# Issuing the four column-position matmuls of the modulation product as one group that waits for its four transfers

## The chip, the cores and the metric

The kernel runs on one core of a Trainium2 chip. The metric is the device time of one execution in microseconds (us): the median of three runs before the change is 3344.96 us (3344.82 to 3346.26). The engines are TensorE (PE in the profile, with PEld for its weight loads), VectorE (DVE), ScalarE (ACT), GpSimd (POOL) and SyncE (SP), which here only issues transfers.

## What is computed

Two transformer blocks of two layers each run over 512 tokens of 1024 features. Nearly all the time goes to products with large weights. The change touches one small product of the second block: per layer, a column vector and its context counterpart are passed through silu and multiplied with a weight of 1024 x 6144, and the result gives shifts, scales and gates.

```python
def modulate(h, shift, scale):
    return h * (1.0 + scale) + shift

silu_c = jax.nn.silu(c)              # c: 1024 features
silu_cc = jax.nn.silu(c_ctx)
for layer in range(DEPTH):           # 2 layers
    mod_x = silu_c @ ada_w[layer] + ada_b[layer]      # ada_w[layer]: 1024 x 6144
    mod_c = silu_cc @ ada_w[layer] + ada_b[layer]
    sh1, sc1, g1, sh2, sc2, g2 = [m[:, None, :] for m in jnp.split(mod_x, 6, axis=-1)]
    csh1, csc1, cg1, csh2, csc2, cg2 = jnp.split(mod_c, 6, axis=-1)
    hx = modulate(rmsnorm(x, norm1_g[layer]), sh1, sc1)
    ...
    x = x + g1 * (mx @ w_out[layer])
```

Neither `c` nor `c_ctx` depends on the first block, so this product can be made long before it is needed.

## The kernel before

`net` emits the parts of the program one after the other: loading, the first mixer (`mixer0`), the modulation and the context beside it, memory attention (`mem_attention`), the MLP, the second mixer, and the second block. A scheduler in the framework then reorders what was emitted: each engine gets one fixed order of instructions, in which an instruction stands where the scheduler's own timing says that its operands are there. On the chip each engine works through its order, and a wait at the head holds up what is queued behind it.

`linear` and `linear_tm` make the large products. `wload` (L227) brings a chunk of weights (tile `raw`, a transfer that SP issues on L237), ACT copies it to `whi` (L241) and DVE forms the rest `wlo` (L242). `mat3` then makes three matmuls in a fast 32-bit format (`hi` and `lo` are halves of the activations). All of them are recorded on L159.

`modulation` (L1001) is emitted through `beside`: with `side` set, its tiles come from a storage of their own, 20 buffers of 128x512 in the tag `b2`, some of which hold other things for long (the memory's keys and values), and its sums go to one PSUM bank, `bank`. It makes six sums one after the other (two layers l, three parts b). Each sum has eight steps k over the 1024 inputs, and each step has four matmuls, one for each 512 columns of the weight. A matmul has the 128x32 tile `sil[:, k]` as weights (two of its 32 columns hold the two vectors) and the 128x512 tile `ada` as moving data, in full 32-bit format; it uses 32 columns of the array. The four of a step stand on the four column positions 0, 32, 64 and 96 (`tile_position=(0, 32 * g)`). So there are 2 x 3 x 8 x 4 = 192 such matmuls (L1023) and 192 transfers of 256 KB (L1022), which SP issues in the same queue as the `raw` transfers. The profile records each of these matmuls as two, so its counts are twice these: "x2" is one matmul, "x8" four. When a sum is done, ACT copies it (`modr`, L1028), PE transposes it (L171), and DVE adds the bias (L1038).

Of the kernel before, what the change touches and what calls it, by code (L numbers as in the profile page):

```python
# [19 lines left out]
KT = 8  # L20
# [35 lines left out]
class Half:  # L56
    """a half of the tokens of a list of pairs of tiles, which may grow"""
# [16 lines left out]
class Stream:  # L74
    """A part of the program that is emitted in steps: it yields how long its next step's operands take,
    or a condition that has to hold before its next step."""
# [5 lines left out]
class Net:  # L82
# [21 lines left out]
    # ---- storage  # L104
# [22 lines left out]
    def b2(self, dt=F32, nm="t", w=T):  # L127
        """a tile of the storage of the streams beside the main one"""
        side, self.side = self.side, True
        t = self.t2(dt, nm, w)  # L130
        self.side = side
        return t
# [22 lines left out]
    # ---- tensor engine  # L155
# [5 lines left out]
    def mat3(self, out, a, b, start, stop, shared=False):  # L161
        """The product of two exact sums of halves, all but that of the low halves.
        shared: other sums are under way in the bank, and only its first matmul has start set."""
        k = {"skip_group_check": True} if shared else {}
        self.mat(out, a[0], b[0], start, False, **k)
        self.mat(out, a[0], b[1], False, False, **k)
        self.mat(out, a[1], b[0], False, stop, **k)
# [5 lines left out]
    # ---- banks that a stream holds over several of its steps  # L173
# [12 lines left out]
    def beside(self, gen):  # L186
        """emits a stream that has storage of its own, which so runs whenever the others wait"""
        self.side = True
        for _ in gen:
            pass  # L190
        self.side = False

    # ---- order of emission: the first stream whose operands should be there goes on
# [32 lines left out]
    # ---- weights: a chunk of up to 1024 columns as an exact sum of two float32r tiles  # L226
# [19 lines left out]
    def linear(self, w, k0, kn, c0, cn, segs, evac, xo=0, apart=0, gate={}):  # L246
        """Feature-major: output tile m has 128 features on partitions and the tokens of a segment.
        segs: (list of (hi, lo), width), narrow segments first; evac(m, tile), or evac(m, tile, segment).
        xo: the inputs begin with this one of a segment's list.
        apart: for so many of the steps of columns (the first if positive, else the last), one segment comes  # L250
        after the other; gate: instructions that are queued before the n-th group of products, by n."""
        nk = kn // 128
        step = min(cn, 256)
        kc = min(nk, (T if self.side else WCH) // step)
        nm = step // 128
        blocks, ns = range(0, nk, kc), cn // step
        order = [(i, kb, s) for i in range(ns) for kb in blocks for s in range(len(segs))]
        n = abs(apart) * len(blocks) * len(segs)
        a = 0 if apart > 0 else len(order) - n
        order[a:a + n] = sorted(order[a:a + n], key=lambda t: t[2])  # L260
        pss, halves, groups = {}, {}, 0
        for at, (i, kb, s) in enumerate(order):
            xs, wd = segs[s]
            if len(xs) < xo + kb + kc:
                yield lambda: len(xs) >= xo + kb + kc
            shared = wd * nm <= T
            if kb == 0:
                yield from self.take("mm", 1 if shared else nm)
                if shared:
                    p = self.mm((128, nm, wd))  # L270
                    pss[i, s] = [p[:, m] for m in range(nm)]
                else:
                    pss[i, s] = [self.mm((128, wd)) for _ in range(nm)]
            if (i, kb) not in halves:
                r0, c = k0 + kb * 128, c0 + i * step
                halves[i, kb] = self.wload(w[r0:r0 + kc * 128, c:c + step], kc, step)
            hi, lo = halves[i, kb]
            ps = pss[i, s]
            for m in range(nm):
                with self.tc.issue_after(gate[groups]) if groups in gate else nullcontext():  # L280
                    for k in range(kb, kb + kc):
                        a = (hi[:, k - kb, sl(m)], lo[:, k - kb, sl(m)])
                        self.mat3(ps[m], a, xs[xo + k], k == 0 and not (shared and m), k == nk - 1, shared)
                groups += 1
            if kb + kc == nk:
                for m in range(nm):
                    evac(i * nm + m, ps[m], *([s] if len(segs) > 1 else []))
                self.give("mm", 1 if shared else nm)
            if s == len(segs) - 1 or order[at + 1][0:2] != (i, kb):
                yield 0.0  # L290

    def halves(self, w, segs, add, swap=False):
        """A product with all of the square w in two parts, that of the first four inputs (the rows of w from
        the middle on, if swap) and that of the others; add(m, tile, last)."""
# [3 lines left out]
    def linear_tm(self, w, k0, kn, c0, cn, xs, ntok, evac, cut=1):  # L298
        """Token-major: 128 tokens on partitions; evac(i, tile of tokens i and features c0...)."""
# [22 lines left out]
    # ---- pieces of norms  # L322
    def rsqrt(self, m):
        """m ** -1/2 of a small tile, refined by a Newton step"""
# [14 lines left out]
    def rows(self, r, n, copy=True):  # L339
        """a value of every token (tokens on partitions, column i for tile i), on all partitions"""  # L340
# [12 lines left out]
    def sq_add(self, st, x, w=T, half=None):  # L353
        """adds x * x to the running tile in the list st, or to a half of it"""
# [9 lines left out]
    def token_rows(self, st, w=T, copy=True):  # L364
        """1/sqrt(mean + eps) of every token, the same on all partitions"""
        return self.rows(self.token_cols(st, w)[1], w // 128, copy)

    def token_cols(self, st, w=T):
        """mean square + eps and its reciprocal root, tokens on partitions: column i for tile i"""
# [7 lines left out]
    def pair(self, w, nm=("hi", "lo")):  # L377
        """room for the two halves of w columns"""
# [5 lines left out]
    def hpair(self):  # L384
        """room for the halves of a normalized tile of the residual stream"""
# [5 lines left out]
    def split(self, x, g=None, w=T, rows=128, pair=None):  # L391
        """x (times a column g) as an exact sum of two float32r tiles"""
# [10 lines left out]
    # ---- residual stream  # L403
# [16 lines left out]
    def add_x(self, m, p, restore=False, norm=None):  # L420
        """x tile m += p; restore: from the order of columns of the grid to that of rows;
        norm: gains (name, layer) of the norm that follows"""
# [16 lines left out]
    # ---- keys and values of the memory  # L439
# [114 lines left out]
    # ---- squared-ReLU MLP of the first block  # L554
# [32 lines left out]
    # ---- first mixer: pooling and latent attention  # L587
    def mixer0(self):
# [81 lines left out]
        def rotate(x, q, rot):  # L670
            """x: tokens of tiles 2 q and 2 q + 1, heads, 32 features, times their gains"""
# [149 lines left out]
    def pipe(self, streams, width):  # L821
        """a stream made of others, of which width are under way at a time"""
# [30 lines left out]
    # ---- second mixer: neighbourhood attention, tokens in the order of columns  # L853
    def mixer1(self):
# [18 lines left out]
        def project(g, o):  # L873
            """queries, keys and values of heads 4 g to 4 g + 3"""
# [126 lines left out]
    # ---- second block: modulation, columns of shift, scale and gate for both streams  # L1001
    def modulation(self):
# [11 lines left out]
        for l in range(2):  # L1014
            mod = self.cst(f"mod{l}", [128, 48, 2])
            for b in range(3):
                yield from self.take("mm")
                p = self.mm()
                for k in range(KT):
                    for g in range(4):  # L1020
                        w = self.t2(nm="ada")
                        nc.sync.dma_start(w, A["ada_w_2"][l, sl(k), b * 2048 + g * 512:b * 2048 + (g + 1) * 512])  # L1022
                        nc.tensor.matmul(p[32 * g:32 * g + 32], lhsT=sil[:, k], rhs=w,  # L1023
                                         start=(k == 0), stop=(k == KT - 1), tile_position=(0, 32 * g))
# [23 lines left out]
    def mod_h(self, l, j, st, xs, sums, w):  # L1048
        """normalized and modulated stream st for sublayer j, as exact halves"""
# [16 lines left out]
    def mod_c(self, l, j):  # L1066
        """mod_h of the context without DVE"""
# [21 lines left out]
    def mod_half(self, l, j, half, h):  # L1089
        """mod_h for a half of the tokens of x"""  # L1090
# [15 lines left out]
    def context(self):  # L1106
        """the context and what its first mixer needs"""
# [22 lines left out]
    # ---- decays of the retention heads and other constants of the scans  # L1130
    def decay_consts(self):
# [19 lines left out]
        # decay of a key to the end (or start) of its chunk  # L1151
# [13 lines left out]
    def decay_tables(self, l):  # L1165
        """decays of a query from its chunk's start (or end), and between query and key in a chunk"""
# [15 lines left out]
    # ---- hybrid mixer: decaying retention and gated linear attention  # L1182
    def hybrid(self, l, h, w, st_in, st_out, outputs, rot, y):
        """the streams of the mixer; its outputs, tiles of 128 features, go to the list y"""
# [35 lines left out]
        def narrow(nm):  # L1220
            """tiles of w columns"""
# [47 lines left out]
        def finish(key, hd, p, ln):  # L1269
            """normalization of a head's output (tokens on partitions), its gate, and back to features"""  # L1270
# [319 lines left out]
    def final(self, half):  # L1590
        """the last norm of a half of the tokens; GpSimd multiplies what DVE has no time for"""
# [18 lines left out]
def shape_tables():  # L1610
    """constants that depend on the shapes alone"""
# [109 lines left out]
```

## Time and profile before

| | |
|---|---|
| median of 3 runs | 3344.96 us |
| span of the profiled execution | 3351.3 us |
| PE busy | 3268.7 us, 98% |
| DVE busy / ACT busy | 1784.2 us, 53% / 1204.7 us, 36% |
| DMA | 323.99 MB, mean 97 GB/s |
| first and last start of a modulation matmul | 191.5 and 483.9 us |

The profiled execution's own time is not listed beside its span; the span is 6.3 us above the median of the runs. A row of the timeline gives the start, the length, the engine, the line, the tiles (written<-read) and a count of instructions that follow each other. The end of a matmul is modelled, so lengths of neighbours overlap; what a matmul takes from the engine is the distance from its start to the start of the next one.

### The profile page before, as it was taken

The page shows a single profiled execution, that of the slowest core. Times are in us where ns is not written, and L with a number is a line of the kernel's source. Part 1 is how long each engine was busy: PE and PEld are TensorE (multiplying, and loading weights), DVE is VectorE, ACT ScalarE, POOL GpSimd, SP SyncE. Part 2 cuts the span into 40 slices and gives each one's busy share as a digit, 9 for nine tenths or more (in the row PEclk, how much of TensorE's full clock was granted, in tenths as well). Part 3 has the DMA queues.
Part 4 walks back from the last instruction along what each step waited for, and adds up shares of the span by engine and source line. Part 5 has one row for each costly group of instructions (what it writes and reads, how often), then busy time and mean ns, then how long its engine had stood idle before and what let it go on. Part 6 is the DMA issues. An engine that isn't in the chain of part 4 may idle for free.

```text
span 3351.3 us, 45020 instructions
## 1 busy us (share of the span) xinstructions
PE 3268.7 (98%) x17942; PEld 2675.4 (80%) x17942; DVE 1784.2 (53%) x3208; ACT 1204.7 (36%) x2157; POOL 207.9 (6%) x257
## 2 busy tenths in 40 slices
PE   8999999999999999999999999999999989899998
PEld 8745448888988778888888987888888879788887
DVE  6853126444555646444776587333334755774444
ACT  5732224222444443222553354221322533433323
POOL 0100000000011100000011212000000011200000
PEclk9999999999999999999999999999999999899999
DMA  5356542332322123333442321222221433123332
GB/s 154 119 165 213 190 149 89 98 97 95 117 60 85 63 67 94 96 99 95 135 121 76 89 83 59 68 63 63 63 63 59 122 89 88 51 64 98 97 94 76
DMA packets 301858, 323.99 MB, mean 97 GB/s; under 512 B 18832, under 2 KB 270608, under 8 KB 301648
## 3 DMA queue, kind: packets, MB, share of 16 engines
q1 hardware_dynamic: 296656, 315.22, 30.9%
q10 hardware_dynamic: 4992, 5.90, 0.6%
q8 instruction: 141, 2.31, 0.3%
q14 instruction: 69, 0.57, 0.1%
HBM read 310.05 MB, written 2.10 MB: 93 GB/s over the span
## 4 chain that ended last, share of the span: by engine, by line
PE 93%; DVE 4%; ACT 1%; DMA 1%; issue 1%; SPq 0%; ACTq 0%; DVEq 0%
PE mm L159 77%; PE pt L159 6%; PE po L159 4%; PE bank L1023 3%; PE pt L171 1%; PE bank L159 1%; DMA raw<-in_w_mem_kv 1%; DVE wlo L242 1%; PE mm L171 0%; DVE S L1444 0%; DVE ht L1057 0%; ACT whi L241 0%; DVE sq L360 0%; DVE o L1289 0%; DMA raw<-in_w_in_e 0%
## 5 line engine op out<-in xcount | busy, mean ns | idle before, releaser
L242 DVE TENSOR_TENSOR wlo<-raw,whi 128x1024 fp32r<-128x1024 f32 (+2 forms) x503 | 598.1, 1190 | 747.5 <-ACT whi L241 724.6
L241 ACT CAST whi<-raw 128x1024 fp32r<-128x1024 f32 (+2 forms) x503 | 504.4, 1005 | 1248.4 <-PE mm L159 1094.4
L159 PE MATMUL mm<-hi,whi 128*128 128x512 f32 (+2 forms) x2768 | 887.1, 358 | 15.4 <-DVE cx L1124 6.1
L159 PE MATMUL mm<-hi,wlo 128*128 128x512 f32 (+2 forms) x2288 | 842.2, 369 | 0.0
L159 PE MATMUL mm<-lo,whi 128*128 128x512 f32 (+2 forms) x1808 | 707.7, 392 | 1.7 <-DVE lo L1062 1.6
L159 PEld LDWEIGHTS mm<-hi,whi 128*128 128x128 f32 (+1 forms) x2768 | 493.9, 190 | 111.3 <-issue 25.0
L159 PEld LDWEIGHTS mm<-hi,wlo 128*128 128x128 f32 (+1 forms) x2288 | 433.4, 189 | 85.8 <-issue 17.0
L159 PE MATMUL mm<-ahi,whi 128*128 128x512 f32 (+1 forms) x1552 | 489.7, 352 | 0.0
L159 PE MATMUL mm<-ahi,wlo 128*128 128x512 f32 (+1 forms) x1296 | 471.8, 366 | 0.0
L159 PEld LDWEIGHTS mm<-lo,whi 128*128 128x128 f32 (+1 forms) x1808 | 340.8, 188 | 87.4 <-issue 17.5
L159 PE MATMUL mm<-alo,whi 128*128 128x512 f32 (+1 forms) x1040 | 399.6, 386 | 0.0
L159 PE MATMUL mm<-whi,hi 128*128 128x256 f32 (+2 forms) x1392 | 367.5, 291 | 17.4 <-ACT v L1196 7.6
L159 PE MATMUL mm<-wlo,hi 128*128 128x256 f32 (+2 forms) x1200 | 346.3, 289 | 2.1 <-DVE wlo L242 2.1
L159 PEld LDWEIGHTS mm<-ahi,whi 128*128 128x128 f32 x1552 | 277.4, 189 | 40.8
L159 PE MATMUL mm<-whi,lo 128*128 128x256 f32 (+2 forms) x1008 | 289.4, 289 | 0.6 <-DVE lo L400 0.6
L159 PEld LDWEIGHTS mm<-whi,hi 128*128 128x128 f32 x1392 | 258.3, 195 | 25.3 <-ACT v L1196 7.8
L159 PEld LDWEIGHTS mm<-ahi,wlo 128*128 128x128 f32 x1296 | 244.4, 189 | 39.4
L159 PEld LDWEIGHTS mm<-wlo,hi 128*128 128x128 f32 x1200 | 234.4, 196 | 10.4 <-issue 6.4
L159 PEld LDWEIGHTS mm<-alo,whi 128*128 128x128 f32 x1040 | 195.5, 188 | 38.3
L159 PEld LDWEIGHTS mm<-whi,lo 128*128 128x128 f32 x1008 | 195.9, 195 | 5.5 <-issue 4.8
L1124 DVE SCALAR_TENSOR_TENSOR x<-mm,mod,x 128x512 f32<-128x512 f32 (+1 forms) x102 | 72.2, 717 | 99.5 <-PE mm L159 99.2
L1023 PE MATMUL bank<-ada,sil 128*32 128x512 f32 x384 | 122.4, 602 | 0.9 <-DMA ada<-in_ada_w 0.9
(320 smaller groups left out, 3254.4 us busy)
## 6 DMA issues: line engine op xcount, KB each, us to landing
raw<-in_w_ff SPq DMA_DIRECT2D x128, 512.0 KB, 3.6
raw<-in_w_mlp SPq DMA_DIRECT2D x128, 512.0 KB, 3.6
raw<-in_w_in SPq DMA_DIRECT2D x98, 512.0 KB, 3.8
ada<-in_ada_w SPq DMA_DIRECT2D x192, 256.0 KB, 3.7
raw<-in_w_qkv SPq DMA_DIRECT2D x24, 512.0 KB, 3.6
raw<-in_w_out SPq DMA_DIRECT2D x24, 512.0 KB, 3.5
raw<-in_w_mem_kv SPq DMA_DIRECT2D x32, 256.0 KB, 3.8
raw<-in_w_mem_q SPq DMA_DIRECT2D x16, 512.0 KB, 3.5
```

Of the source, the lines that this page charges most:

```text
L159: return self.nc.tensor.matmul(out, lhsT=lhsT, rhs=rhs, start=start, stop=stop, **k).ins
L171: self.nc.tensor.transpose(out, in_, self.ident)
L241: nc.scalar.copy(hi[:, v], raw[:, v])
L242: nc.vector.tensor_sub(lo[:, v], raw[:, v], f32(hi[:, v]))
L1023: nc.tensor.matmul(p[32 * g:32 * g + 32], lhsT=sil[:, k], rhs=w, start=(k == 0), stop=(k == KT - 1), tile_position=(0, 32 * g))
L1124: self.nc.vector.scalar_tensor_tensor(x, p, self.mod[l][:, 16 + 24 * j + m, st:st + 1], x, ALU.mult, ALU.add)
```

## The change

In each step k the four `ada` tiles are allocated and their four transfers issued first, then the four matmuls follow. `wait_for` makes the first matmul of the four wait for the other three transfers too (its own it waits for anyway). Removed comments make up the rest of the diff; the line numbers in the rows of after below are higher by 6 to 9.

```diff
+    def wait_for(self, ins, *others):
+        for o in others:
+            self.tc.add_manual_dep(ins, o.name, mybir.DependencyInfo(mybir.DependencyClass.Sync,
+                                                                     mybir.DependencyReason.DATA))
...
                 for k in range(KT):
-                    for g in range(4):
-                        w = self.t2(nm="ada")
-                        nc.sync.dma_start(w, A["ada_w_2"][l, sl(k), b * 2048 + g * 512:b * 2048 + (g + 1) * 512])
-                        nc.tensor.matmul(p[32 * g:32 * g + 32], lhsT=sil[:, k], rhs=w,
-                                         start=(k == 0), stop=(k == KT - 1), tile_position=(0, 32 * g))
+                    ws, loads = [self.t2(nm="ada") for _ in range(4)], []
+                    for g, w in enumerate(ws):
+                        c0 = b * 2048 + g * 512
+                        loads.append(nc.sync.dma_start(w, A["ada_w_2"][l, sl(k), c0:c0 + 512]).ins)
+                    first = None
+                    for g, w in enumerate(ws):
+                        m = nc.tensor.matmul(p[32 * g:32 * g + 32], lhsT=sil[:, k], rhs=w,
+                                             start=(k == 0), stop=(k == KT - 1), tile_position=(0, 32 * g)).ins
+                        first = first or m
+                    self.wait_for(first, *loads[1:])
                     self.pe += 900
                     yield 2500
```

What the scheduler makes of it is seen in PE's order. Before, in the first products of `mem_attention(0)` (`mm_3903`, `mm_3904` are its queries in PSUM; `bank_3327` is the third of the six sums), the modulation's matmuls stand alone between two or three others:

```order
L159 MATMUL mm_3903<-hi_3047,whi_3936 128x512
L1023 MATMUL bank_3327<-ada_3361,sil_3102 32x512
L159 MATMUL mm_3903<-lo_3048,whi_3936 128x512
L159 MATMUL mm_3903<-hi_3047,wlo_3937 128x512
L1023 MATMUL bank_3327<-ada_3364,sil_3102 32x512
L159 MATMUL mm_3903<-hi_3087,whi_3936 128x512
L159 MATMUL mm_3903<-lo_3088,whi_3936 128x512
L1023 MATMUL bank_3327<-ada_3367,sil_3102 32x512
L159 MATMUL mm_3903<-hi_3087,wlo_3937 128x512
```

In the changed kernel, in the same sum and the same stage, they stand in fours:

```order
L159 MATMUL mm_3974<-hi_2944,wlo_3977 128x512
L1032 MATMUL bank_3327<-ada_3352,sil_3102 32x512
L1032 MATMUL bank_3327<-ada_3353,sil_3102 32x512
L1032 MATMUL bank_3327<-ada_3354,sil_3102 32x512
L1032 MATMUL bank_3327<-ada_3355,sil_3102 32x512
L159 MATMUL mm_3974<-hi_2951,whi_3976 128x512
L159 MATMUL mm_3974<-lo_2952,whi_3976 128x512
L159 MATMUL mm_3974<-hi_2951,wlo_3977 128x512
L159 MATMUL mm_3974<-hi_2991,whi_3976 128x512
L159 MATMUL mm_3974<-lo_2992,whi_3976 128x512
L159 MATMUL mm_3974<-hi_2991,wlo_3977 128x512
L159 MATMUL mm_3974<-hi_2999,whi_3976 128x512
```

The matmuls that stood alone have come together, and the stretches of other work between them have grown. Over the whole program the 192 matmuls stand in 106 unbroken runs before and in 45 after: 33 runs of four, five of eight, one of six, one of five, two of three and three of one. (The scheduler still broke three of the 48 groups up, early in the modulation; two runs close on each other make a five or an eight.)

On SP's queue the transfers of the modulation keep their number and stand between the same `raw` transfers, a few places earlier or later. Before, at the start of the third sum:

```order
L1022 DMA ada_3355<-in_ada_w 128x512
L237 DMA raw_3975<-in_w_mem_q 128x4x256
L237 DMA raw_4053<-in_w_mem_q 128x4x256
L1022 DMA ada_3358<-in_ada_w 128x512
L237 DMA raw_4107<-in_w_mem_q 128x4x256
L237 DMA raw_4199<-in_w_mem_q 128x4x256
L1022 DMA ada_3361<-in_ada_w 128x512
```

and after:

```order
L243 DMA raw_4107<-in_w_mem_q 128x4x256
L1029 DMA ada_3328<-in_ada_w 128x512
L1029 DMA ada_3329<-in_ada_w 128x512
L1029 DMA ada_3330<-in_ada_w 128x512
L1029 DMA ada_3331<-in_ada_w 128x512
...
L1029 DMA ada_3353<-in_ada_w 128x512
L243 DMA raw_4199<-in_w_mem_q 128x4x256
L1029 DMA ada_3354<-in_ada_w 128x512
L243 DMA raw_4253<-in_w_mem_q 128x4x256
L1029 DMA ada_3355<-in_ada_w 128x512
```

Here two `raw` transfers have come between the four transfers of one group.

## Rows read from the trace of the kernel before

**Rows 1.** Page: busy time by engine, then the chain that ended last by engine
```profile
PE 3268.7 (98%) x17942; PEld 2675.4 (80%) x17942; DVE 1784.2 (53%) x3208; ACT 1204.7 (36%) x2157; POOL 207.9 (6%) x257
...
PE 93%; DVE 4%; ACT 1%; DMA 1%; issue 1%; SPq 0%; ACTq 0%; DVEq 0%
```

**Rows 2.** Busy time in the modulation's stretch: window, PE, PEld, DVE, ACT, POOL, clock, DMA
```profile
185.00:495.00 310.00, 309.09 (x1204) 142.93 (x1203) 102.17 (x229) 81.29 (x163) 0.00 (x0) 1.00 0.58 186
```

**Rows 3.** PE timeline, 301 to 311 us: start, length, what, count
```profile
301.62 0.39 PE L159 MATMUL mm<-hi,whi 128*128 128x512 f32 x1
301.85 0.39 PE L159 MATMUL mm<-lo,whi 128*128 128x512 f32 x1
...
304.19 0.40 PE L159 MATMUL mm<-hi,whi 128*128 128x512 f32 x1
304.51 1.05 PE L1023 MATMUL bank<-ada,sil 128*32 128x512 f32 x2
305.49 0.50 PE L159 MATMUL mm<-lo,whi 128*128 128x512 f32 x1
305.82 0.39 PE L159 MATMUL mm<-hi,wlo 128*128 128x512 f32 x1
306.05 0.40 PE L159 MATMUL mm<-hi,whi 128*128 128x512 f32 x1
306.38 1.05 PE L1023 MATMUL bank<-ada,sil 128*32 128x512 f32 x4
307.36 0.50 PE L159 MATMUL mm<-lo,whi 128*128 128x512 f32 x1
```

**Rows 4.** PE timeline, 218 to 229 us: a run of eight and one of four
```profile
218.94 1.92 PE L1023 MATMUL bank<-ada,sil 128*32 128x512 f32 x16
220.80 0.55 PE L171 MATMUL mm<-ident,P 128*128 128x128 f32 x3
...
227.08 1.06 PE L1023 MATMUL bank<-ada,sil 128*32 128x512 f32 x8
228.07 1.07 PE L159 MATMUL po<-PT,v 128*64 128x512 f32 x2
```

**Rows 5.** PE timeline: the first run, one between single-column products, the last run
```profile
191.47 2.78 PE L1023 MATMUL bank<-ada,sil 128*32 128x512 f32 x22
194.18 1.07 PE L159 MATMUL po<-PT,v 128*64 128x512 f32 x2
...
404.34 0.72 PE L159 MATMUL pt<-one,sq 128*128 128x1 f32 x6
405.00 1.04 PE L1023 MATMUL bank<-ada,sil 128*32 128x512 f32 x2
405.98 0.38 PE L159 MATMUL pt<-one,sq 128*128 128x1 f32 x2
406.29 1.04 PE L1023 MATMUL bank<-ada,sil 128*32 128x512 f32 x2
...
483.47 1.04 PE L1023 MATMUL bank<-ada,sil 128*32 128x512 f32 x2
```

**Rows 6.** Page: all modulation matmuls: busy and mean ns, idle before them, releaser
```profile
L1023 PE MATMUL bank<-ada,sil 128*32 128x512 f32 x384 | 122.4, 602 | 0.9 <-DMA ada<-in_ada_w 0.9
```

**Rows 7.** Transfers of the tile ada: issues from 190 us on; all issues; waits; landing
```profile
L1022 SPq DMA_DIRECT2D ada<-in_ada_w x181: 327/328/1589, 192.5 to 467.9; - x181
...
L1022 SPq DMA_DIRECT2D ada<-in_ada_w x192: 327/328/1589, 157.7 to 467.9; - x192
  PEld bank L1023: 7.0, 17
DMA to landing us min/median/max: 2.6/3.7/6.9
```

**Rows 8.** SP's waits, 150 to 500 us: who waited for whom, us, times, longest
```profile
SPq L1022 <- PE bank L1023: 128.9, 84, 6.8
SPq L237 <- DVE wlo L242: 41.6, 8, 11.7
```

**Rows 9.** DMA traffic, 185 to 495 us, and GB/s in 40 slices of 192.5 to 207
```profile
DMA packets 36090, 57.63 MB, mean 186 GB/s; under 512 B 3424, under 2 KB 12651, under 8 KB 36075
...
GB/s 0 0 28 203 243 373 333 288 277 249 311 305 249 277 220 294 266 220 288 356 379 407 407 401 413 401 407 396 367 390 333 136 271 237 277 96 73 0 0 0
```

**Rows 10.** Busy time, 297 to 330 us, columns as in rows 2
```profile
297.00:330.00 33.00, 33.00 (x96) 10.92 (x95) 3.80 (x4) 4.85 (x7) 0.00 (x0) 1.00 0.72 228
```

## The prediction

> **What bounds the kernel now.** I read the page's busy times and its chain of work that ended last first: PE is busy for 98% of the span, and 93% of the chain is PE's [rows 1]. So what a stage costs is what it takes from PE, as long as PE finds work. Then I read the stretch in which the modulation runs: from 185 to 495 us PE is busy for 309.09 of 310 us at the full clock (1.00, the 2.4 GHz level), while DVE has 102 us of work there and ACT 81 [rows 2]. In this stretch PE alone sets the pace, and whatever time is taken out of PE's order comes out of the kernel, until transfers or another engine are late. Last I read PE's timeline there, for what one modulation matmul takes from PE alone and in company.
>
> **What a run of modulation matmuls costs.** Starts are compared, since ends are modelled. One alone: from 304.51 to the next start at 305.49, 0.98 us. Two in a row: 306.38 to 307.36, again 0.98 us [rows 3]. Four: 227.08 to 228.07, 0.99 us; eight: 218.94 to 220.80, 1.86 us [rows 4]; eleven: 191.47 to 194.18, 2.71 us [rows 5]. So up to four matmuls on four positions take the time of one, and each further round of four adds about 0.87 us; a run of n takes 0.98 us for the first round and 0.87 us for each begun round after it.
>
> A run also costs something at its edges. Two ordinary matmuls start 0.23 us apart (301.62, 301.85). The one ahead of a run is followed only after 0.32 us (304.19 to 304.51), and the first one behind it takes 0.33 us (305.49 to 305.82) [rows 3]: 0.09 + 0.10 = 0.19 us for each run. Between single-column products the edges are cheaper: six of them and an edge take 0.66 us (404.34 to 405.00), so about 0.11 each; two of them between two runs take 0.31 us, 0.09 more than 2 x 0.11 [rows 5].
>
> **The change part by part.**
>
> *Removed: lone runs.* In the timeline from the first run at 191.47 to the last at 483.47 [rows 5] I count 106 runs: 82 of one matmul, 11 of two, 2 of three, 2 of four, and 9 of six to eleven. Their sum by starts: 82 x 0.976 = 80.0, 11 x 0.982 = 10.8, 2 x 0.989 = 2.0, the two fours 0.99 and 2.90 (the second holds the one wait for data of 0.9 us [rows 6] and was broken into two rounds by it), one six 1.84, three sevens 5.5, two eights 3.7, one nine 2.69 and two elevens 5.4: together 115.9 us. The page's 122.4 us of busy time for this line [rows 6] is the same with the modelled tails (some 0.07 us for each of 106 runs).
>
> *Added: fours.* In the changed order there are 45 runs: 33 of four x 0.996 = 32.9, five of eight x 1.855 = 9.3, a six 1.84, a five about 1.83, two threes 2.0 and three ones 2.9: together 50.7 us. Gain in the runs themselves: 115.9 - 50.7 = 65 us.
>
> *Edges.* 106 - 45 = 61 runs fewer. At 0.19 us this is 11.6 us, at 0.09 us 5.5 us; most lone runs stood among the large matmuls, so I take 11.6, call it 12.
>
> A rule speaks against the first term. The Trainium skill, "TensorE: Matmul & The Clock Gate", Part 3 (packing small matmuls), says that a weight load overlaps a running matmul only where the two use different row groups; the four positions here differ in columns only. By it four in a row would cost four times one, an estimate of 3.9 us; the row of four shows 0.99 us [rows 4], so the trace does not bear it out here.
>
> *The wait that is added.* The first matmul of a group now waits for four landings instead of one, and everything on PE stands behind it: the products of `mem_attention(0)`, and behind those ACT and DVE, which free the weight buffers for the next `raw` transfers. What covers it is the lead of the transfers. 11 of the 192 issues lie ahead of the first matmul (192 - 181), and from then on the loads mostly wait for a buffer that a modulation matmul gives back, 84 times, 128.9 us in all [rows 7, 8]: there are 11 buffers. With 11, the last tile of a group goes into a buffer of the group two before it, so its issue comes when that group is done. With 77 us gone, 48 groups come in about 218 us (295 - 77), 4.5 us apart. Two distances less one run of 1.0 us leave 8 us, against a landing 3.7 us after the issue (median; 2.6 to 6.9) [rows 7]. The order is uneven, though: at the tightest places I see, eight large matmuls, a run and eight small products (8 x 0.23 + 1.0 + 1.1, with edges some 4.3 us) lie between the two, less than the slowest landing. Before, 17 weight loads waited for data for 7.0 us, nearly all of it beneath a running matmul: PE itself idled 0.9 us [rows 6, 7]. I take 2 us of new idle time, from nothing up to 10 us (four places at the 6.9 - 4.3 = 2.6 us of a slow landing).
>
> *Semaphores, order and the rest.* The transfers are the same 192; the extra semaphore instructions sit on PE's queue ahead of work that is not waited for, at no cost while a matmul runs. The scheduler also reshuffles a few dozen instructions in the second block, where the waits are of a few us each; I see no side to it and allow 5 us either way. DVE and ACT have 102 and 81 us of work [rows 2] in what would be some 235 us, so neither becomes the bound; the same is true of the one PSUM bank, whose six copies and transposes stay.
>
> *Sum.* 65 + 12 - 2 = 75 us off the profiled span of 3351.3. The span is 6.3 us above the median of the runs; I take the same 75 off the median: 3345 - 75 = 3270 us.
>
> **Rivals.**
>
> *Transfers become the bound.* The stretch moves 57.63 MB [rows 9]. In bursts the engines reach some 400 GB/s [rows 9], at which this takes 144 us, far below the 233 us that would be left of 310. But if the mixture of `raw` and `ada` with its gaps holds no more than the 228 GB/s of the busiest long window (DMA share 0.72) [rows 10], it takes 253 us, and the gain stops at 57 us, and with a few us of gaps near 53: about 3292 us. Against it: that window was limited by buffers given back one at a time, not by the engines. Chance 7%.
>
> *The four do not overlap.* If a matmul's weights were not loaded beneath one that runs on another column position, or if the waits pulled the four apart on PE, four would cost 4 x 0.98 us and only the edges would be saved: 3345 - 12 = 3333 us. Against it stand the rows of two, four, eight and eleven [rows 3 to 5]. That the order doesn't hold fours can be excluded, since 45 runs are counted. Chance 2%. (The Trainium skill's rule on row groups, "TensorE: Matmul & The Clock Gate", Part 3, would give this case.)
>
> *Slower: the group waits behind a `raw` transfer.* SP issues in order. A `raw` transfer waits for a buffer that DVE frees (8 times, 41.6 us, up to 11.7 us each [rows 8]), and a few groups' transfers now have one or two `raw` transfers between them. If PE stands at such a group, the products that would free the raw buffer stand behind the group, on PE, and the wait feeds on itself. It decides from the point where these stalls exceed the 77 us gained: eight stalls of 9.6 us. With eight at the longest wait seen, 94 us, the time is 3345 - 77 + 94 = 3362 us. Against it: the matmuls that free a `raw` buffer belong to an earlier chunk than those queued behind the group, and today's waits of SP leave PE idle for 0.9 us only. Chance 3%.
>
> **How the numbers follow.** The forecast has 87%, the bound by transfers 7%, no overlap 2%, slower 3%, and 1% for others near no change. The forecast's own range: the least, 65 + 5.5 - 10 - 5 = 55 us off, gives 3290; the most, edges of 0.25 us (15 us) with no wait and 5 us from the later order, 85 us off, gives 3260. That is at the lower edge of the second case, and about 15% lie outside, so the range is 3260 to 3290. Chances: faster by over 0.2% (6.7 us, about what a measurement of this kernel can tell from no change) 0.96, within it 0.01, slower 0.03.
>
> **What would show it.** In the profile of the changed kernel the modulation line should be busy for some 54 us (50.7 and the tails) instead of 122.4, in about 45 runs, "x8" rows that take 1.0 us from start to start. The chain should lose about 2 points on that line. Idle time of PE on that line, waiting for the tile `ada`, should be a few us; if it is over 10, the term of the wait is wrong; if "x8" rows take 2 us or more, the first term is. SP should still wait mostly for modulation matmuls. PE's busy time should fall by about 76 us and DVE's stay at 1784; if PE idles more in the second block, the order there has cost something that I left out.

## The result, and the profile after

The changed kernel takes 3271.8 us (median; 3269.8 to 3278.9) against 3344.9 us (3343.6 to 3346.3) of the kernel before on the same chip: a ratio of 0.9779, 95% interval 0.9766 to 0.9792, some 73 us less. The forecast was 3270 us, 3260 to 3290. The profiled execution after has a span of 3277.2 us, 74.1 us less than the 3351.3 of before; it was the longest of the four runs after, and the span before, too, lies above the median of its runs.

From the page of the changed kernel, the answers to [rows 1] and [rows 6]: busy time by engine, the chain that ended last by engine and by line, and the modulation matmuls (now line 1032) with their idle time.

```profile
PE 3195.6 (98%) x17942; PEld 2669.8 (81%) x17942; DVE 1787.2 (55%) x3208; ACT 1204.8 (37%) x2157; POOL 206.9 (6%) x257
...
PE 93%; DVE 3%; ACT 1%; DMA 1%; issue 1%; SPq 0%; ACTq 0%; DVEq 0%
PE mm L159 79%; PE pt L159 6%; PE po L159 4%; PE bank L1032 2%; PE pt L171 1%; PE bank L159 1%; DMA raw<-in_w_mem_kv 1%; PE mm L171 0%; DVE wlo L248 0%; DVE S L1455 0%; DVE sq L366 0%; ACT whi L247 0%; DVE o L1300 0%; DVE ht L1068 0%; DMA a
...
L1032 PE MATMUL bank<-ada,sil 128*32 128x512 f32 x384 | 53.9, 603 | 0.5 <-DMA ada<-in_ada_w 0.5
```

PE's busy time fell by 73.1 us and DVE's stayed (1784.2 before). The same 384 records of modulation matmuls (192 matmuls, two records each) now keep PE busy for 53.9 us instead of 122.4, and PE idles 0.5 us for their data instead of 0.9. PE is as full as before: the work went, no new wait came.

The modulation's stretch after, the answer to [rows 2] (window, PE, PEld, DVE, ACT, POOL, clock, DMA share, GB/s); this window ends 15 us ahead of the modulation. The two rows below it are parts of the stretch. Then the transfers of its weights, the answer to [rows 7]:

```profile
185.00:418.00 233.00, 232.45 (x1181) 138.03 (x1180) 100.84 (x222) 78.92 (x157) 0.00 (x0) 0.99 0.71 235
300.00:418.00 118.00, 118.00 (x616) 74.09 (x609) 39.33 (x94) 34.62 (x76) 0.00 (x0) 0.99 0.78 261
303.80:307.20 3.40, 3.40 (x10) 2.69 (x10) 0.65 (x4) 0.41 (x2) 0.00 (x0) 0.50 0.81 266
```

```profile
L1032 PE MATMUL bank<-ada,sil x384: 589/592/617, 191.9 to 432.8; 128*32 128x512 f32 x192
L1029 SPq DMA_DIRECT2D ada<-in_ada_w x192: 327/382/1610, 158.1 to 424.3; - x192
...
  PEld bank L1032: 2.1, 6
...
DMA to landing us min/median/max: 2.6/4.5/7.0
```

The modulation now starts at 191.9 and its last matmul at 432.8, 51 us earlier than before (483.9). Over 233 us PE is busy for all but 0.55 us. Nearly the same transfers flow in less time, at 235 GB/s with the DMA engines busy for 0.71 (186 and 0.58 before, [rows 2]); the median landing rose from 3.7 to 4.5 us after the issue. PE's weight loads still waited less for them: 6 times, 2.1 us, against 17 times, 7.0 us.

The clock of this stretch is 0.99 and not the 1.00 of before, because for 3.4 us from 303.80 the granted clock was 0.50 (the 1.2 GHz level), while PE had work all the time; the profile before shows nothing of the kind up to 985 us. Fourteen matmuls there, and sixteen of the same kind before at the full clock (next starts: 308.60 and 334.18):

```profile
303.71 4.95 PE L159 MATMUL pt<-mk,q 128*128 128x256 f32 x14
```

```profile
330.83 3.70 PE L159 MATMUL pt<-mk,q 128*128 128x256 f32 x16
```

Fourteen take 4.89 us where sixteen took 3.35. Half of the 3.4 us, 1.7 us, is lost by this. (What else is longer there is the edge of the run behind them.) None of the other six profiles of this document shows such a stretch between the first modulation matmul and the place that is compared next, so it is not taken for an effect of the change; why it came is open.

Two groups on PE's timeline after, beside [rows 3] (start, length, what, count; "x8" is four matmuls with two records each):

```profile
296.24 0.39 PE L159 MATMUL mm<-hi,wlo 128*128 128x512 f32 x1
296.56 1.07 PE L1032 MATMUL bank<-ada,sil 128*32 128x512 f32 x8
297.55 0.50 PE L159 MATMUL mm<-hi,whi 128*128 128x512 f32 x1
297.89 0.39 PE L159 MATMUL mm<-lo,whi 128*128 128x512 f32 x1
...
299.60 1.07 PE L1032 MATMUL bank<-ada,sil 128*32 128x512 f32 x8
300.59 0.50 PE L159 MATMUL mm<-hi,wlo 128*128 128x512 f32 x1
```

Four take 0.99 us from start to start (296.56 to 297.55; 299.60 to 300.59), what one took alone before, and the edges are those of before: 0.32 us ahead of the run and 0.34 behind it instead of 0.23.

Where the 74.1 us are is read from two places that both orders share. First the same matmul a good way behind the modulation, a `po` product that waits for the tile `PT`, in the kernel before and then in the one after:

```profile
988.78 0.44 PE L159 MATMUL po<-PT,v 128*64 128x128 f32 x4 [0.97 <-ACT PT L969]
```

```profile
913.78 0.44 PE L159 MATMUL po<-PT,v 128*64 128x128 f32 x4 [0.97 <-ACT PT L975]
```

Then a product near the end, before and after:

```profile
3338.91 0.61 PE L159 MATMUL pt<-mean,sq 128*128 128x1 f32 x4 [2.41 <-DVE sq L360]
```

```profile
3264.71 0.60 PE L159 MATMUL pt<-mean,sq 128*128 128x1 f32 x4 [2.41 <-DVE sq L366]
```

At the first place the gain is 988.78 - 913.78 = 75.0 us, at the second 74.2. So all of it is made ahead of the first place, and 0.8 us was given back behind it.

### The profile page after: what moved, and what is told of

Its sections match the earlier page's. It is cut to its first block, busy times and chain, and to the rows that moved or that the text cites. A ratio compares the mean times of both kernels' runs of the same rounds, so it can differ in the third digit from the quotient of the medians.

```text
span 3277.2 us, 45112 instructions
## 1 busy us (share of the span) xinstructions
PE 3195.6 (98%) x17942; PEld 2669.8 (81%) x17942; DVE 1787.2 (55%) x3208; ACT 1204.8 (37%) x2157; POOL 206.9 (6%) x257
## 4 chain that ended last, share of the span: by engine, by line
PE 93%; DVE 3%; ACT 1%; DMA 1%; issue 1%; SPq 0%; ACTq 0%; DVEq 0%
PE mm L159 79%; PE pt L159 6%; PE po L159 4%; PE bank L1032 2%; PE pt L171 1%; PE bank L159 1%; DMA raw<-in_w_mem_kv 1%; PE mm L171 0%; DVE wlo L248 0%; DVE S L1455 0%; DVE sq L366 0%; ACT whi L247 0%; DVE o L1300 0%; DVE ht L1068 0%; DMA ada<-in_ada_w 0%
## 5 line engine op out<-in xcount | busy, mean ns | idle before, releaser
L952 POOL TENSOR_TENSOR bm<-bias,mask 128x192 f32<-128x192 f32 (+1 forms) x64 | 45.5, 735 | 839.5 <-DMA mask<-in_na_mask 643.6
```

The lines of the kernel that those rows point to most:

```text
L952: nc.gpsimd.tensor_add(bm[:, sl(hh, 256)][:, :n], o.tab[hp * 2 + hh][:, f0:f0 + n], masks[(0, 1, 1, 2)[b]][:, f0:f0 + n])
```

## The experiments

The theory: a run of up to four matmuls on the four column positions costs PE what one costs, and each run costs a little at its edges; the wait only serves to make runs of four, and is itself covered by the lead of the transfers. The rivals are other sources of the gain (the transfers issued four in a row, fewer changes between kinds of matmul) and costs that are hidden here by luck (transfers, buffers). Five kernels, each an edit of the changed kernel and timed against the kernel before.

**The transfers in fours, without the wait.**

```
-                    self.wait_for(first, *loads[1:])
```

> The changed kernel without the added wait: the four tiles are still allocated and loaded ahead of their four matmuls, but each matmul waits for its own transfer alone. The scheduler then puts the matmuls back into 106 runs, as in the kernel before. Theory (the time is set by how many runs the 192 matmuls form): 115.9 us of runs again, time 3345 us, within 0.2% of the kernel before. Rival (issuing the transfers in fours is what helps): near 3272 us.

Measured: 3348.1 us (3346.1 to 3355.9) against 3347.0, ratio 1.0001 (0.9992 to 1.0011). From its page, the modulation matmuls:

```profile
L1032 PE MATMUL bank<-ada,sil 128*32 128x512 f32 x384 | 122.4, 602 | 0.9 <-DMA ada<-in_ada_w 0.9
```

Busy and idle time are those of [rows 6] to the last digit, and PE has the 106 runs of before. Writing the loads and matmuls in fours moves nothing: the scheduler pulls the matmuls apart again. All of the gain hangs on the wait.

**Fours on one column position.** The wait and the order stay; the four matmuls of a group share a position, and the position changes with each step of `k`.

```
+                        o = 32 * (k % 4)
-                        m = nc.tensor.matmul(p[32 * g:32 * g + 32], lhsT=sil[:, k], rhs=w,
-                                             start=(k == 0), stop=(k == KT - 1), tile_position=(0, 32 * g)).ins
+                        m = nc.tensor.matmul(p[o:o + 32], lhsT=sil[:, k], rhs=w, start=(k < 4 and g == 0),
+                                             stop=(k >= 4 and g == 3), tile_position=(0, o)).ins
```

> The changed kernel with the four matmuls of a step all on one column position (32 x (k mod 4)) instead of four different ones; the sums are then not those of the reference, all transfers, waits and counts stay. 43 runs. Theory (the gain is that four positions work at once): each matmul now takes its own 0.87 us, 192 x 0.87 = 166 us and about 5 us for the ends of 43 runs, less some 6 us where a run goes over to the next position, so 165 instead of 50.7 us and a time of 3272 + 114 = 3386 us, slower than the kernel before. Rival (what counts is that there are fewer runs, 43 instead of 106, whatever stands in them): about 3272 us, since the runs and edges are as few as in the changed kernel.

Measured: 3376.7 us (3374.3 to 3378.2), ratio 1.0085 (1.007 to 1.01): slower than before. Its modulation matmuls on the page, then a run of four and a run of eight on its PE timeline:

```profile
L1033 PE MATMUL bank<-ada,sil 128*32 128x512 f32 x384 | 159.4, 595 | 0.0
```

```profile
282.39 3.62 PE L1033 MATMUL bank<-ada,sil 128*32 128x512 f32 x8
285.94 0.96 PE L159 MATMUL mm<-hi,whi 128*128 128x512 f32 x3
...
288.21 5.37 PE L1033 MATMUL bank<-ada,sil 128*32 128x512 f32 x16
293.51 0.50 PE L159 MATMUL mm<-hi,whi 128*128 128x512 f32 x1
```

Four on one position take 3.55 us (282.39 to 285.94), 0.98 for the first and 0.86 for each further one; four on four positions take 0.99. So the gain is the positions' working side by side, not the row of four. (The edit moves the sum in PSUM together with the position, so it doesn't tell the two apart.) Fewer runs alone (43 instead of 106) don't make up for it. The expected time was some 9 us too long: the runs of eight, which hold two positions, overlap in part, 5.30 us instead of 7.1, and I had allowed 6 us for this in all where it gave about 14.

**Groups of two.** The wait stands behind two transfers instead of four.

```
-                    ws, loads = [self.t2(nm="ada") for _ in range(4)], []
+                    for g0 in (0, 2):
+                        ws, loads = [self.t2(nm="ada") for _ in range(2)], []
...
+                        self.wait_for(first, *loads[1:])
```

> Groups of two: the first matmul of a pair waits for both transfers. 67 runs (53 of two, five of four, the rest longer or odd). Theory: runs 53 x 0.98 and the rest 22.5, 74.6 us instead of 50.8, and 22 edges more at 0.16 us, 3.5 us: 3272 + 27 = 3299 us. Rival (any grouping gives most of the gain, because the wait clears the order of the rest): within 5 us of 3272.

Measured: 3299.7 us (3296.1 to 3304.1), ratio 0.9856 (0.9841 to 0.9871), 47 us off, as expected. From its page and its PE timeline:

```profile
L1033 PE MATMUL bank<-ada,sil 128*32 128x512 f32 x384 | 79.2, 603 | 0.0
```

```profile
300.61 1.05 PE L1033 MATMUL bank<-ada,sil 128*32 128x512 f32 x4
301.59 0.50 PE L159 MATMUL mm<-hi,wlo 128*128 128x512 f32 x1
```

A pair takes 0.98 us. There are 67 runs, 74.5 us by starts instead of 115.9; halving the width of a group gives back about a third of the gain. Of the 96 pairs 53 stand alone; the others have come to stand side by side, in 14 runs of three to ten.

**Groups of eight.** Two steps of `k` behind one wait for eight transfers.

```
-                for k in range(KT):
-                    ws, loads = [self.t2(nm="ada") for _ in range(4)], []
+                for k2 in range(0, KT, 2):
+                    ws, loads = [self.t2(nm="ada") for _ in range(8)], []
```

> Groups of eight, two steps k at a time: the first of eight matmuls waits for all eight transfers, of 11 buffers. 32 runs, 20 of them of eight. Theory: runs 51.6 us (20 x 1.86 and the rest), 13 edges fewer at 0.16 us, 2 us: 3271 us, the same as the changed kernel within 0.2%, if the waits stay covered. Rival (the wait is not covered: with eight tiles in use only three of the next group can be loaded ahead, and the other five land at least 2.6 + 4 x 0.66 = 5.2 us after the group's end): PE idles 1 to 3 us at each of 24 groups, 3295 to 3340 us.

Measured: 3273.6 us (3270.5 to 3278.8), ratio 0.9779 (0.9764 to 0.9795), the ratio of fours. From its page, its PE timeline and its transfers:

```profile
L1033 PE MATMUL bank<-ada,sil 128*32 128x512 f32 x384 | 53.7, 599 | 0.0
```

```profile
294.45 1.92 PE L1033 MATMUL bank<-ada,sil 128*32 128x512 f32 x16
296.31 0.50 PE L159 MATMUL mm<-hi,whi 128*128 128x512 f32 x1
```

```profile
DMA to landing us min/median/max: 2.7/4.7/7.2
```

Eight take 1.86 us, two rounds, as in [rows 4]. Runs went from 45 to 32, which by the edges should have brought about 2 us. The medians can't tell that, and the traces don't show it either (722.1 us to the marker against 721.9, see the table of kernels below). Even a wait for eight of eleven buffers leaves PE without idle time on this line. The groups stand further apart, and the modulation lasts to 472.8 us instead of 432.8.

**Seven buffers instead of eleven.** Four of the eleven are held by idle tiles from before the modulation to its end.

```
+        hold = [self.t2(nm="hold") for _ in range(4)]
+        for h in hold:
+            nc.gpsimd.memset(h, 0.0)
...
+        for h in hold:
+            nc.gpsimd.tensor_mul(h[:, 0:1], h[:, 0:1], mod[:, 47, 0:1])
```

> The changed kernel with four of the modulation's 11 tile buffers held by idle tiles until the modulation is done (8 small GpSimd operations more): 7 buffers. A group's last transfer now waits for the group just before it. The scheduler spreads the groups over a longer stretch: 50 runs, 45 of them of four. Theory (PE idles only where the transfers are late, and the longer stretch gives them time): runs 49.7 us, 5 edges more, 1 us, idle time on the modulation line up to 5 us: 3270 to 3280 us. Rival (the wait for four is covered by the 11 buffers alone): a landing 3.7 us after the issue of the last of four is not covered, 1 to 2 us at each of 48 groups, 3320 to 3370 us.

Measured, on another chip: 3284.3 us (3279.2 to 3286.6) against 3348.6 us, ratio 0.9803 (0.9787 to 0.982). From its page, then the `po` product of above, which serves as a marker, then one of PE's longest waits from 2000 us on (who waited for whom: us, times, longest):

```profile
L1035 PE MATMUL bank<-ada,sil 128*32 128x512 f32 x384 | 53.2, 604 | 3.4 <-DMA ada<-in_ada_w 3.4
```

```profile
917.72 0.44 PE L159 MATMUL po<-PT,v 128*64 128x128 f32 x4 [0.97 <-ACT PT L975]
```

```profile
PE pt L171 <- DVE gb L1409: 5.6, 1, 5.6
```

The new wait shows now, but only 3.4 us of it in three places. The marker comes 3.9 us later than in the changed kernel (917.72 against 913.78), and the wait on `gb`, 1.1 us there, is 5.6 us here; PE's order behind the marker is another one too. The median is 4 us beyond the 3280 us that were expected at the most; the 3320 to 3370 us of a chain of stalls did not come. The experiment doesn't separate buffers from order, though: with seven buffers the scheduler spread the same groups up to 561 us, some 7.7 us apart ((561.4 - 191.9) / 48) where eleven gave 5.0 ((432.8 - 191.9) / 48).

## Why the prediction was right, by its own steps

| step | forecast | measured |
|---|---|---|
| runs, 115.9 to 50.7 us | 65 | 65.2 (by starts after) |
| edges, 61 runs fewer | 12 (bound 5.5) | 12.4 |
| idle time after, from the added wait | -2 (0 to -10) | -0.5 |
| half clock, 303.8 to 307.2 us | not foreseen | -1.7 |
| first modulation matmul 0.4 us later | not foreseen | -0.4 |
| order in the second block | 0 (-5 to +5) | -0.8 |
| sum, against the profiled span | 75 | 74.1 |

The two large terms came as they were worked out. That the sum is met within 1 us is in part luck: 1.5 us that the wait did not cost stand against 2.9 us that nobody foresaw or that were put at nothing.

**The runs.** Their number and sizes come from the order and held; so did the price of each, 0.98 us for a first round of up to four and 0.87 for a further one. The Trainium skill's rule that a weight load overlaps a running matmul only where the row groups differ ("TensorE: Matmul & The Clock Gate", Part 3) is not what this chip shows here. The weight loads (PEld) of the four at 296.56, and one of those in the run of four at 282.39 on one position:

```profile
296.55 0.16 PEld L1032 LDWEIGHTS bank<-ada,sil 128*32 128x32 f32 x8 [0.35 <-DMA ada<-in_ada_w]
```

```profile
282.85 0.11 PEld L1033 LDWEIGHTS bank<-ada,sil 128*32 128x32 f32 x1 [0.32 <-issue]
```

All eight loads of the four, which share their rows, are done 0.16 us after the start of a run of 0.99 us. On one position, too, a load of 0.11 us lies beneath matmuls that follow each other without a gap, and still four take 3.55 us. So the price hangs on whether the matmuls themselves run at the same time, and not on the loads. The prediction read more into the rule than it says: the table of the same part has three column positions at 2.38 times the speed, so the page as a whole does not make four cost four times one.

**The edges** were sized rightly for fours. From the first modulation matmul to the marker the stretch is 75.4 us shorter. The runs give 65.2 us of it (the 0.9 us that PE idled before lie within one of the runs). Added to the 10.2 us that are left, the 0.5 us of idle time after and the 1.7 us of the half clock make 12.4 us for 61 runs, 0.20 each against the forecast 0.19. The same reckoning for the other kernels, from the starts on their timelines:

| kernel | runs, us by starts | first matmul to marker, us | shorter by | runs' gain | left for the edges, each | gain in medians |
|---|---|---|---|---|---|---|
| before | 106, 115.9 | 191.47 to 988.78 | | | | |
| one position | 43, 156.4 | 191.76 to 1015.13 | -26.1 | -40.5 | 14.4, 0.23 | -29.7 |
| pairs | 67, 74.5 | 190.68 to 939.60 | 48.4 | 41.4 | 7.0, 0.18 | 47.3 |
| fours (the change) | 45, 50.7 | 191.87 to 913.78 | 75.4 | 65.2 | 12.4, 0.20 | 73.1 |
| eights | 32, 51.4 | 191.32 to 913.43 | 75.2 | 64.5 | 10.7, 0.14 | 73.4 |
| seven buffers | 50, 49.7 | 191.95 to 917.72 | 71.5 | 66.2 | 8.8, 0.16 | 64.3 |

For seven buffers the 3.4 us of idle time are added to what is left. So an edge is not one price: it lies between 0.14 and 0.23 us, and the cheap edges of [rows 5] show that it goes by what stands around the run. What the medians lack beside the stretch to the marker is 1 to 4 us in the first four. With seven buffers it is 7.2 us: 4.5 are the longer wait on `gb`, and the rest stays open. Its four runs were granted a clock of 0.983 to 0.987, the seven of the kernel before on that chip 0.986 to 0.988, which may be part of it.

**The wait** cost less than forecast, 0.5 us instead of 2. What was off is the tight place, where a slow landing was to outlast 4.3 us of work: it occurred once at most, for 0.5 us, though landings became slower, to 4.5 us in the median. SP's waits after, from 150 to 440 us, the answer to [rows 8] (which goes to 500 us), say that the cover had not shrunk:

```profile
SPq L1029 <- PE bank L1032: 85.0, 39, 7.2
SPq L243 <- DVE wlo L248: 43.5, 14, 8.5
```

SP still waits mostly for modulation matmuls to give buffers back, 85.0 us in 39 waits, so issues come as early as the buffers allow. But my reason for it, eleven buffers and so a lead of two groups, is not the whole of it: with seven of them PE waited for only 3.4 us. What was left out is the spacing: for eights and with seven buffers the scheduler set the groups further apart. How much of the cover is buffers and how much is spacing was not separated.

**The rivals.** *Transfers become the bound* falls: the stretch ran at 235 GB/s, a little above the 228 that this rival took as the most [rows 10], with 0.5 us of idle time, and 118 us of it at 261 GB/s with PE busy throughout. *The four do not overlap* falls by the timeline after, and by the kernel with one position, which comes nearest to it: 3377 us. The 3333 us of the rival were reckoned wrongly. The runs of before hold overlaps of their own (115.9 us for 192 matmuls); at 0.98 us for each, all 192 would take 188 us, 72 more than before, and with 12 us of edges the rival's time would be about 3405 us. *The group waits behind a `raw` transfer* falls: up to 440 us SP waited for `raw` buffers 14 times, for 43.5 us, no longer than 8.5 us each. Before, up to 515 us, the same place of the program by the gain of 75 us, it was 10 times, 57.0 us, up to 11.7. PE hardly noticed.

**What was to be seen**: 54 us busy (53.9), fours of 1.0 us (0.99), PE's busy time down by 76 (73.1), DVE's unchanged (+3.0). The chain's share of the line went from 3% to 2% where two points were expected; the page rounds, and 122.4 and 53.9 us of the spans are 3.7 and 1.6%.

## What to carry to other kernels

Where PE sets the pace, cost a small matmul by its run and not by itself: compare starts on the timeline, alone and in company, and multiply by the runs that the order really holds. Matmuls on different column positions only share their time when nothing stands between them in PE's order; a scheduler that takes each as its data lands pulls them apart, and an extra dependency of the first on all their transfers puts them together. Such a wait is cheap as long as buffers and spacing keep the transfers ahead; look at the queue's waits and PE's idle time on that line to see whether they do.

## What the runs showed of the hardware that was not expected

A transfer's median landing rose from 3.7 us before to 4.5 (fours), 4.6 (pairs) and 4.7 (eights), while the longest went only from 6.9 to at most 7.2; with seven buffers it was 3.8 and on one position, where the same transfers had more time, 3.0. That more transfers in a row make them slower would fit, but was not tested by itself; the median doesn't simply follow the traffic (214 GB/s over the modulation for the eights, 235 for the fours). And a run of eight on two positions took 5.30 us, less than two fours on one position (7.1) and more than the 3.5 us at which two positions would run wholly side by side. Its sixteen weight loads, two for each matmul, start one by one 0.43 us apart at the beginning and at the end of the run and two by two in the middle: four of the eight matmuls had company, which makes six rounds, 0.98 + 5 x 0.86 = 5.3 us.
